# Two-operand elementwise work moved from GpSimd to VectorE in a one-core encoder step

## The chip, the cores and the metric

The kernel runs on one core of one Trainium2 chip. The metric is the device time of one execution in microseconds (us). A core has a matrix engine (TensorE, PE in the profile; its weight loads are the row PEld), three engines for elementwise work (VectorE, DVE; ScalarE, ACT; GpSimd, POOL) and queues for DMA, of which this kernel uses that of SyncE (SP). Each engine executes its own instructions in the order in which the program gives them; semaphores order them between engines.

## The reference, cut to what matters

One inference step of a two-layer streaming encoder on 544 tokens: 512 of a new stream (prompt) and 32 that continue a running one (sample). The width is 1024. Each layer is a half-step gated FFN, a token mixer, and another half-step FFN; layer 0 mixes by retention, layer 1 by differential attention against keys and values that are projected once, after layer 0. Around every sub-layer stand two norms:

```python
h = modulate(x, g_norm[l, 0], mod[:, 0], mod[:, 1])       # rms_norm(x) * g * (1 + scale) + shift
x = x + HALF * mod[:, 2, None] * rms_norm(swiglu(h, w_ffn_in[l, 0], w_ffn_out[l, 0]), g_norm[l, 1])
h = modulate(x, g_norm[l, 2], mod[:, 3], mod[:, 4])
y, st = retention_mixer(h, ...)                           # layer 1: diff_mixer
x = x + mod[:, 5, None] * rms_norm(y, g_norm[l, 3])
h = modulate(x, g_norm[l, 4], mod[:, 6], mod[:, 7])
x = x + HALF * mod[:, 8, None] * rms_norm(swiglu(h, w_ffn_in[l, 1], w_ffn_out[l, 1]), g_norm[l, 5])
```

with `rms_norm(y, g) = y * rsqrt(mean(y * y) + eps) * g`, `swiglu(h) = (silu(a) * b) @ w_out` for `a, b = split(h @ w_in)`, and a rotary embedding on queries and keys: `[x1 * cos - x2 * sin, x2 * cos + x1 * sin]`. The modulations `mod` are products of the conditioning vectors with a large matrix. Everything is float32.

## The kernel before, in words

**Layout.** Activations stand feature-major: 8 tiles of 128 features by 544 tokens in `X`. The tokens are worked in two halves, the first with 256 tokens, the second with 288 (256 of the prompt and the 32 of the sample). A product of one 128-wide column block of a weight matrix with one half is a unit; there are 368 units, each done for both halves.

**Products in three parts.** TensorE multiplies in a fast format (`F32R`) that keeps fewer bits, so both operands are split in a high and a low part, and a unit is three products for each of its 6 or 8 blocks of K: high x high, high x low, low x high (`run_unit`, L604). Weights arrive by DMA on SP's queue into one of three raw buffers (`w_dma`); `w_conv` then *stages* them: ScalarE rounds them to the high part (L581), and a subtraction makes the low part (L585 on VectorE or L586 on GpSimd), which lets the raw buffer go. Four staged buffers (`NW`) exist. 544 stagings serve the 368 units: where both halves use a unit's weights soon after one another they are staged once, otherwise twice.

**What follows a product.** ScalarE and VectorE take it out of PSUM: silu and gate in the FFNs (L926, L927, L930, L939, L942), the split of the result into parts (L906, L907), the sum of the output product over parts (L893, L895), the rotary embedding (`rot`: L997 and L1001 on VectorE with one operand in PSUM, then the addition of the two, L1005, on GpSimd), and in retention two decay multiplications of queries (L1242, L1275, GpSimd).

**Ends of sub-layers** (`sub_end`, `x_norm`). `sq_sum` squares the 8 tiles on ScalarE (L812, L815) and adds them up on VectorE (L817). `rstd` sums over features with TensorE (L709), scales (L713, VectorE), takes the power -1/2 on GpSimd (L715) and spreads it over the partitions with TensorE (L720). Then VectorE scales each tile of y (L854), and the residual addition X + z follows (L859 on GpSimd or L860 on VectorE). The next norm squares and sums the new X alike, and `pre_ops` makes the next operand of it (L747 VectorE, L756 ScalarE, L762 VectorE). Retention and attention take more powers on GpSimd (L1134, L1585).

**The order.** While the program is built, a planner (`Sched`) lays all of it out on an estimated clock. Every piece of work is a small process that asks for an engine with an estimated cost and a priority; an engine that is free by the estimate takes the ready item of the lowest number, and the instruction is emitted at that moment. So each engine's order is fixed before the run. Norms ask with 0 to 2, work after products with 15 to 20, the low part of a staging with `FIN_P = 25`. `plan` puts the units in order: around the ends of sub-layers the first half is some units ahead, so that products of one half run while the norm of the other is worked out.

Two of the items are alternatives (`"ALT"`): offered to two engines at once, with 1000 added to the priority on the second, and done by whichever takes it first. Staging offers its subtraction to VectorE, then GpSimd. The residual addition, reversed by `[::XADD]` with `XADD = -1`, does the same. The planner's cost of a two-operand instruction of n elements is `(64 + n) / 0.96` ns on VectorE and `150 + 2.1 * n` on GpSimd. Its estimate has no term for one engine holding up another.

Of the kernel before, what the change touches and what calls it, by code (L numbers as in the profile page):

```python
# [29 lines left out]

# columns of the constant table
C_ID = 0
# [5 lines left out]
C_N = 220  # L38
# columns of the per-head decay table
T_DM = 0  # L40
# [3 lines left out]

# lead of the first half, delay of a wakeup, staged weights kept free for the products that come next
L0 = 1
# [4 lines left out]
def _path():  # L51
    """Where each half stands: the first one is ahead around the ends of the sub-layers, so that the products of one
    half run while the norms, or the attention, of the other are worked out."""
    p = [((None, L0), (None, 0))]
    for e in ((0, 1), (0, 2), "kv", (1, 0)):
        x, hold, y, z = BND.get(e, BND0)
        p += [((e, -z), (e, -z - L0)), ((e, 0), (e, -x)), ((e, 0), (e, -x + hold)), ((e, y), (e, 0)),
              ((e, y + z), (e, y + z - L0))]
    return p + [((e0, a), (e1, b)) for e0, a, e1, b in ATT]
# [60 lines left out]
class Sched:  # L120
    """Orders the instructions: small processes compete for the engines on an estimated clock."""

# [146 lines left out]

def c_pool(n):  # L270
    return 150 + 2.1 * n


class Operand:
    """A 128 x 544 operand, in two token halves, each split into two float32r parts."""

# [30 lines left out]
class Load:  # L307
    """One staging of a unit's weights, for one token half or for both."""

# [16 lines left out]
def yoco_step(ctx: ExitStack, tc: tile.TileContext, I, O):  # L326
# [68 lines left out]

    def pool(n, fn, pr=None):
        return ("POOL", c_pool(n), fn) if pr is None else ("POOL", c_pool(n), fn, pr)

    def dma(nbytes, out, in_, pr=None, eng=None):
# [3 lines left out]

# [1 line left out]
    ready = {n: Ev() for n in ("ct", "vt", "sc", "lam")}  # L405
# [32 lines left out]

# [1 line left out]
    # modulation m: 0..8 layer 0, 9..10 shared kv, 11..19 layer 1  # L440
    mod_ev = [[Ev() for _ in range(4)] if m < 2 else Ev() for m in range(20)]
# [27 lines left out]
    def ada_first():  # L469
        """The first two modulations, a quarter of their features at a time."""  # L470
        for q in range(4):
# [64 lines left out]
    def derive(i, kind, m, gcol, mul):  # L536
        """DRV[i] = (1 + mod) * g, or (mul * mod) * g"""
        drv_ev[i] = [Ev() for _ in range(4)] if m < 2 else Ev()
# [14 lines left out]

# [1 line left out]
    units = []  # L555
# [15 lines left out]
    def w_conv():  # L571
        for d in loads:
            w = (yield ("get", wpool, 1))[0]
            d.w = w
            yield d.raw_ev
            nk = d.unit.nk
            n = nk * P
            hi = WT[w][:, 0, :nk, :].rearrange("p k f -> p (k f)")
            lo = WT[w][:, 1, :nk, :].rearrange("p k f -> p (k f)")
            src = fa(d.raw)  # L580
            yield act(n, lambda: nc.scalar.copy(hi, src))  # L581

            def fin(d=d, hi=hi, lo=lo, src=src, n=n):
                yield ("ALT", [
                    ("DVE", c_dve(n), lambda: nc.vector.tensor_tensor(lo, src, hi.bitcast(F32), ALU.subtract)),  # L585
                    ("POOL", c_pool(n), lambda: nc.gpsimd.tensor_tensor(lo, src, hi.bitcast(F32), ALU.subtract))])  # L586
                S.put(rawbuf, d.rawbuf)
                S.set(d.staged)
            go(fin(), FIN_P)

# [1 line left out]
    def run_unit(u, H, b):  # L592
# [48 lines left out]
    def plan():  # L641
        """The order of the products along a path of (units of the first half, of the second), and which weights are
        staged twice."""
        marks["end"] = n = len(units)
# [50 lines left out]

# [1 line left out]
    def blocks(H):  # L697
        return ((0, P), (P, P)) if H == 0 else ((0, P), (P, P), (2 * P, NS_TOK))

    def rstd(acc, H, dim, pr=0):  # L700
        """Per-token rstd of the column sums of acc, broadcast over partitions in a PSUM bank."""
        nb, n = (3, 96) if H else (2, P)
# [26 lines left out]
    def pre_ops(H, Rb, n, gi, mi, ops, q=1):  # L729
        """h = x * rstd * gs + shift, split into operands."""  # L730
        if mi:
# [41 lines left out]
    class YBuf:  # L773
        """Holds a sub-layer's y, 8 tiles, while it is accumulated."""

# [23 lines left out]
    def sq_sum(H, src, evs, acc):  # L799
        """acc = sum over the 8 tiles of src squared"""  # L800
        c = COLS[H]
# [32 lines left out]
    def sub_end(H, yevs, gg, nexts, final=False):  # L834
# [10 lines left out]
        for f in range(8):  # L845
# [3 lines left out]
            def one(f=f, ze=ze):  # L849
                z = yield from get(n, -4)  # L850

                def a():
# [4 lines left out]
                S.set(ze)  # L857
                yield ("ALT", [
                    ("POOL", c_pool(n), lambda: nc.gpsimd.tensor_tensor(X[:, f, c], X[:, f, c], fa(z), ALU.add)),  # L859
                    ("DVE", c_dve(n), lambda: nc.vector.tensor_tensor(X[:, f, c], X[:, f, c], fa(z), ALU.add))][::XADD])  # L860
                free(z)
# [20 lines left out]

# [1 line left out]
    def out_stage(w, k0, ops, first, last, yevs):  # L884
# [16 lines left out]
    def split_ops(H, src, op, pr=20):  # L901
        """op = hi, lo of the float32 columns src"""
        c = COLS[H]
# [6 lines left out]
    def ffn(l, j, hops, yevs):  # L910
        w_in, w_out = I["w_ffn_in"][l][j], I["w_ffn_out"][l][j]
        parts = ((0, 8), (8, 16), (16, 22))
        for pi, (f0, f1) in enumerate(parts):
            st = Stage(hops if pi == 2 else [])
            gops = [Operand() for _ in range(f1 - f0)]
            for f in range(f0, f1):
# [3 lines left out]
                def post_a(H, b, sil=sil, sev=sev):  # L920
# [3 lines left out]
                    if l in TANH:  # L924
                        # 2 silu(a) = (1 + tanh(a / 2)) a: tanh shares a table with exp
                        yield act(n, lambda: nc.scalar.activation(fa(t), PS[b][:, :n], AF.Tanh, scale=0.5))  # L926
# [22 lines left out]

# [1 line left out]
    ret = {}  # L951
# [16 lines left out]
    def piece(h, nm):  # L968
        """A buffer of a head, taken by its first use."""
        hd = heads[h]  # L970
# [20 lines left out]
    def rot(H, b, rr, dst, pr=20):  # L991
        """Rotates a projected tile, whose partner rows lie 64 apart, by the table rr."""
        c = COLS[H]
# [10 lines left out]
        put_bank(b)  # L1004
        yield pool(n, lambda: nc.gpsimd.tensor_tensor(dst, a1, a2, ALU.add), pr)  # L1005
        free(t1)
# [99 lines left out]
    def ret_head(h, oo):  # L1106
# [11 lines left out]
        def finish(b, H, c0, n):  # L1118
            """o in bank b, token-major: group norm, gate, split"""
            blks = ((0, P), (P, P)) if n == 256 else ((0, n),)  # L1120
# [114 lines left out]
        def sample():  # L1235
# [5 lines left out]
            c0 = NP_TOK  # L1241
            yield pool(NS_TOK, lambda: nc.gpsimd.tensor_tensor(fa(qs, NS_TOK), V("q")[:, c0:c0 + NS_TOK],  # L1242
                                                               V("t")[:, T_QS:T_QS + NS_TOK], ALU.mult))
            b = yield from bank(miscb)
# [29 lines left out]
        qd = yield from get(256)  # L1274
        yield pool(256, lambda: nc.gpsimd.tensor_tensor(fa(qd), V("q")[:, 256:512], V("t")[:, T_QD:T_QD + 256], ALU.mult))  # L1275
        unpiece(h, "q", "t")
# [16 lines left out]

# [1 line left out]
    kv = {"k": [Ev(2) for _ in range(8)], "v": [Ev(2) for _ in range(8)], "rope_ev": Ev(), "left": 16}  # L1295
# [8 lines left out]
    def to_tok(H, src, h):  # L1304
        """Stores a feature-major tile of the values token-major."""
        b = yield from bank(miscb)
# [49 lines left out]

# [1 line left out]
    at = {}  # L1358
# [131 lines left out]
    def at_block(h, H, ii):  # L1490
        """The queries 128 i .. 128 (i + 1) of a head"""
        i = 2 * H + ii
# [33 lines left out]

        # the first 64 queries don't see the last 64 keys
        def mask():
# [187 lines left out]

# [1 line left out]
    go(setup(), 0)  # L1718
# [4 lines left out]

    # DRV indices: l * 10 + 2 * s (pre of sub-layer s), l * 10 + 2 * s + 1 (post), 6: kv pre
    for l in range(2):
# [25 lines left out]
    for l in range(2):  # L1751
        m0 = 11 * l
        for s in range(3):
            if l or s:
                mark((l, s))
            # the last modulation of this sub-layer and the first ones of the next
            ada_due.append((max(0, len(units) + ADA_LEAD), 6 if l == 0 and s == 2 else (m0 + 3 * s + 4) // 2))
# [30 lines left out]

# [1 line left out]
ROPE_LEAD = 30  # L1790
# [3 lines left out]
W_P = {0: 0.5, 1: 1.5, 2: 2.5}  # L1794
# layers whose silu is worked out by tanh
TANH = (1,)
FIN_P = 25
CONV_P = 3
NEXT_P = 25
XADD = -1  # L1800
ADA_HI = 900
# [8 lines left out]

# [1 line left out]
# Rows of a rotary tile: all first halves of the heads' dimensions, then all second halves.  # L1812
def _rope(d, reps, scale=1.0):
# [43 lines left out]
def _cols(w):  # L1857
    """[.., K, N] -> [.., N / 128, 128 (of K), K / 128 * 128]"""
    *b, K, N = w.shape
# [5 lines left out]
def _pairs(w):  # L1865
    """The columns of each pair of 64-wide heads: both first halves, then both second halves"""
    *b, N = w.shape
# [54 lines left out]
```

## Time and profile before

| what | before |
| --- | --- |
| median of 3 runs | 2639.63 us (2636.75 to 2639.95) |
| span of the profiled execution | 2637.7 us, 1.9 us below that median; no other time is listed for it |
| TensorE busy | 2540.7 us, 96% |
| VectorE busy | 1362.2 us, 52% |
| ScalarE busy | 1037.5 us, 39% |
| GpSimd busy | 425.1 us, 16% |
| staging subtractions | 433 on VectorE (L585), 111 on GpSimd (L586) |
| rotary additions on GpSimd (L1005) | 64, 55.6 us |
| residual additions | 52 on VectorE (L860), 44 on GpSimd (L859) |

Busy times are those of the profiled execution; engines run side by side, so they don't add up to the span. A row of a group gives the source line, the engine, the operation, what it writes and reads, its count, then the busy time and the mean duration of one in ns, then the idle time of the engine just before and what ended it. `FA` is the large scratch area in SBUF, `w` the staged weights, `r` the operands of the products, `ps` PSUM.

### The profile page before, as it was taken

To read this page: it belongs to the slowest core of one execution; us is meant where nothing else is said; L and a number is where in the kernel's file an instruction comes from. 1 tells how busy PE (TensorE), PEld (TensorE's weight loads), DVE (VectorE), ACT (ScalarE), POOL (GpSimd) and SP (SyncE) were. 2 spreads that over 40 slices of the span, in tenths; PEclk is the share of its full clock that TensorE was granted. 3 is DMA by queue.
4 is the path that set the end of the run, shared out by engine and by line. 5 is a ranking of instruction groups with operands and counts; after the bars stand their busy time and mean duration, and the time that the engine had idled before them with its cause. 6 is when DMAs were issued, how large, how long until landed. Compare 5 with 4: busy or idle time off the path is not lost.

```text
span 2637.7 us, 48412 instructions
## 1 busy us (share of the span) xinstructions
PE 2540.7 (96%) x19908; PEld 2399.0 (91%) x19908; DVE 1362.2 (52%) x2481; ACT 1037.5 (39%) x2055; POOL 425.1 (16%) x323
## 2 busy tenths in 40 slices
PE   7999999899999989999999899999999899999998
PEld 5799999799999987899998799999789888889998
DVE  5223336844333365223338734556766966668555
ACT  3222224443323333222224433434554565544433
POOL 1000002422202121000003420000441433322000
PEclk9999999999999999999999999999999999999999
DMA  8722324642222238622225753555664444445553
GB/s 323 270 87 89 97 89 136 225 134 94 76 90 79 75 109 304 221 86 95 88 79 168 257 164 111 169 176 187 237 226 147 139 164 169 160 143 172 168 165 109
DMA packets 119549, 400.57 MB, mean 152 GB/s; under 512 B 13344, under 2 KB 31904, under 8 KB 109088
## 3 DMA queue, kind: packets, MB, share of 16 engines
q1 hardware_dynamic: 119328, 397.48, 44.5%
q8 instruction: 156, 2.56, 0.4%
q14 instruction: 65, 0.53, 0.1%
HBM read 384.19 MB, written 13.24 MB: 151 GB/s over the span
## 4 chain that ended last, share of the span: by engine, by line
PE 82%; DVE 11%; issue 3%; DMA 2%; ACT 1%; POOL 1%; SPq 0%; DVEq 0%; POOLq 0%; ACTq 0%
PE ps L604 73%; DVE FA L817 2%; DVE r L762 2%; PE ps L508 2%; DMA FA<-in_ada 2%; DVE FA L854 1%; PE ps L1524 1%; DVE FA L747 1%; DVE X L860 1%; PE ps L1566 1%; DVE w L585 1%; ACT w L581 1%; DMA X<-in_xb 0%; PE ps L720 0%; PE ps L1197 0%
## 5 line engine op out<-in xcount | busy, mean ns | idle before, releaser
L604 PE MATMUL ps<-r,w 128*128 128x288 f32 (+1 forms) x17280 | 2286.9, 292 | 14.7 <-DVE r L762 6.5
L604 PEld LDWEIGHTS ps<-r,w 128*128 128x128 f32 x17280 | 2216.5, 192 | 83.5 <-issue 56.3
L581 ACT CAST w<-FA 128x1024 fp32r<-128x1024 f32 (+1 forms) x544 | 556.3, 1023 | 907.5 <-PE ps L604 829.1
L585 DVE TENSOR_TENSOR w<-FA,w 128x1024 fp32r<-128x1024 f32 (+1 forms) x433 | 521.7, 1205 | 597.2 <-ACT w L581 596.0
L586 POOL TENSOR_TENSOR w<-FA,w 128x1024 fp32r<-128x1024 f32 (+1 forms) x111 | 262.8, 2369 | 974.3 <-DVE r L907 366.3
L715 POOL TENSOR_TENSOR FA<-FA,NHALF 128x2 f32<-128x2 f32 (+1 forms) x24 | 23.9, 995 | 829.5 <-DVE FA L713 791.8
L942 DVE TENSOR_TENSOR FA<-ps,FA 128x256 f32<-128x256 f32 (+1 forms) x88 | 38.6, 441 | 186.6 <-PE ps L604 184.7
L906 ACT CAST r<-FA 128x256 fp32r<-128x256 f32 (+1 forms) x176 | 73.1, 417 | 129.7 <-DVE FA L942 92.9
L895 DVE TENSOR_TENSOR FA<-ps,FA 128x288 f32<-128x288 f32 (+1 forms) x144 | 62.6, 438 | 102.1 <-PE ps L604 100.8
L817 DVE TENSOR_TENSOR FA<-FA 128x256 f32<-128x256 f32 (+1 forms) x168 | 104.5, 623 | 12.9 <-ACT FA L815 11.7
L907 DVE TENSOR_TENSOR r<-FA,r 128x256 fp32r<-128x256 f32 (+1 forms) x176 | 87.7, 499 | 24.0 <-ACT r L906 23.5
L762 DVE SCALAR_TENSOR_TENSOR r<-FA,MOD,r 128x256 fp32r<-128x256 f32 (+1 forms) x168 | 94.6, 619 | 0.7 <-ACT r L756 0.3
L756 ACT ACTIVATE r<-FA,MOD 128x256 fp32r<-128x256 f32 (+1 forms) x168 | 61.9, 436 | 66.1 <-DVE FA L747 65.8
L508 PE MATMUL ps<-FA,SC 128*32 128x512 f32 x576 | 77.1, 612 | 3.1 <-DMA FA<-in_ada 3.0
L1005 POOL TENSOR_TENSOR FA<-FA 128x256 f32<-128x256 f32 (+1 forms) x64 | 55.6, 869 | 144.2 <-DVE FA L1001 142.0
L939 DVE SCALAR_TENSOR_TENSOR FA<-ps,FA 128x256 f32<-128x256 f32 (+1 forms) x88 | 38.6, 439 | 56.1 <-PE ps L604 55.2
L997 DVE TENSOR_TENSOR FA<-ps,FA 128x256 f32<-128x256 f32 (+1 forms) x64 | 28.0, 438 | 69.9 <-PE ps L604 67.8
L930 ACT ACTIVATE FA<-ps 128x256 f32<-128x256 f32 (+1 forms) x88 | 34.5, 394 | 71.4 <-PE ps L604 69.9
L747 DVE SCALAR_TENSOR_TENSOR FA<-X,DRV,ps 128x256 f32<-128x256 f32 (+1 forms) x168 | 56.3, 395 | 8.9 <-PE ps L720 8.5
L1001 DVE TENSOR_TENSOR FA<-ps,FA 64x256 f32<-64x256 f32 (+1 forms) x128 | 56.1, 438 | 2.3
L709 PEld LDWEIGHTS ps<-ONE,FA 128*32 128x32 f32 x408 | 6.9, 121 | 53.6 <-DVE FA L817 48.9
L815 ACT ACTIVATE FA<-X 128x256 f32<-128x256 f32 (+1 forms) x84 | 33.7, 426 | 53.5 <-DVE X L860 48.0
(147 smaller groups left out, 1271.0 us busy)
## 6 DMA issues: line engine op xcount, KB each, us to landing
FA<-in_w_ffn_in SPq DMA_DIRECT2D x256, 512.0 KB, 3.2
FA<-in_ada SPq DMA_DIRECT2D x80, 1024.0 KB, 6.8
FA<-in_w_ffn_out SPq DMA_DIRECT2D x95, 512.0 KB, 3.5
FA<-in_w_in_a SPq DMA_DIRECT2D x60, 512.0 KB, 3.2
FA<-in_w_ffn_out SPq DMA_DIRECT2D x61, 384.0 KB, 3.1
FA<-in_w_kv SPq DMA_DIRECT2D x22, 512.0 KB, 3.6
FA<-in_w_out_a SPq DMA_DIRECT2D x19, 512.0 KB, 3.3
FA<-in_w_q_b SPq DMA_DIRECT2D x16, 512.0 KB, 3.3
```

The lines of the kernel that those rows point to most:

```text
L508: te.matmul(PS[b][32 * g:32 * g + 32, :], lhsT=SC[:, k, :], rhs=fa(ada_buf[u, k], 512, g * 512), start=(k == 0), stop=(k == 7))
L581: yield act(n, lambda: nc.scalar.copy(hi, src))
L585: ("DVE", c_dve(n), lambda: nc.vector.tensor_tensor(lo, src, hi.bitcast(F32), ALU.subtract)),
L586: ("POOL", c_pool(n), lambda: nc.gpsimd.tensor_tensor(lo, src, hi.bitcast(F32), ALU.subtract))])
L604: te.matmul(PS[b][:, :n], lhsT=w[:, a, k, :], rhs=x, start=(k == 0 and j == 0), stop=(k == u.nk - 1 and j == 2))
L747: nc.vector.scalar_tensor_tensor(fa(z, c1 - c0, o), X[:, f, c0:c1], DRV[:, gi, f, s:s + 1], PS[Rb][:, o:o + c1 - c0], ALU.mult, ALU.mult)
L756: nc.scalar.activation(op.hi(H, c0, c1), fa(z, c1 - c0, o), AF.Identity, bias=MOD[:, mi, f, s:s + 1])
L762: nc.vector.scalar_tensor_tensor(op.lo(H, c0, c1), fa(z, c1 - c0, o), MOD[:, mi, f, s:s + 1], op.hi(H, c0, c1).bitcast(F32), ALU.add, ALU. ...
L817: yield dve(n, lambda: nc.vector.tensor_tensor(acc, acc, fa(t), ALU.add))
L895: yield dvp(n, lambda: nc.vector.tensor_tensor(Y[:, f, c], PS[b][:, :n], Y[:, f, c], ALU.add), 15)
L906: yield act(n, lambda: nc.scalar.copy(op.hi(H), src), pr)
L907: yield dve(n, lambda: nc.vector.tensor_tensor(op.lo(H), src, op.hi(H).bitcast(F32), ALU.subtract), pr)
```

## The change

GpSimd keeps the powers alone. The staging subtraction and the residual addition are no longer offered to two engines but asked of VectorE; the rotary addition and the two decay multiplications of retention go to VectorE with VectorE's cost in the estimate. Priorities stay as they are, and the planner works out a new order with them. Comments are also taken out, which changes line numbers little.

```diff
@@ w_conv
             def fin(d=d, hi=hi, lo=lo, src=src, n=n):
-                yield ("ALT", [
-                    ("DVE", c_dve(n), lambda: nc.vector.tensor_tensor(lo, src, hi.bitcast(F32), ALU.subtract)),
-                    ("POOL", c_pool(n), lambda: nc.gpsimd.tensor_tensor(lo, src, hi.bitcast(F32), ALU.subtract))])
+                yield dve(n, lambda: nc.vector.tensor_tensor(lo, src, hi.bitcast(F32), ALU.subtract))
                 S.put(rawbuf, d.rawbuf)
                 S.set(d.staged)
@@ sub_end
                 S.set(ze)
-                yield ("ALT", [
-                    ("POOL", c_pool(n), lambda: nc.gpsimd.tensor_tensor(X[:, f, c], X[:, f, c], fa(z), ALU.add)),
-                    ("DVE", c_dve(n), lambda: nc.vector.tensor_tensor(X[:, f, c], X[:, f, c], fa(z), ALU.add))][::XADD])
+                yield dve(n, lambda: nc.vector.tensor_tensor(X[:, f, c], X[:, f, c], fa(z), ALU.add))
                 free(z)
@@ rot
-        yield pool(n, lambda: nc.gpsimd.tensor_tensor(dst, a1, a2, ALU.add), pr)
+        yield dve(n, lambda: nc.vector.tensor_tensor(dst, a1, a2, ALU.add), pr)
@@ ret_head, sample
-            yield pool(NS_TOK, lambda: nc.gpsimd.tensor_tensor(fa(qs, NS_TOK), V("q")[:, c0:c0 + NS_TOK],
-                                                               V("t")[:, T_QS:T_QS + NS_TOK], ALU.mult))
+            yield dve(NS_TOK, lambda: nc.vector.tensor_tensor(fa(qs, NS_TOK), V("q")[:, c0:c0 + NS_TOK],
+                                                              V("t")[:, T_QS:T_QS + NS_TOK], ALU.mult))
@@ ret_head
-        yield pool(256, lambda: nc.gpsimd.tensor_tensor(fa(qd), V("q")[:, 256:512], V("t")[:, T_QD:T_QD + 256], ALU.mult))
+        yield dve(256, lambda: nc.vector.tensor_tensor(fa(qd), V("q")[:, 256:512], V("t")[:, T_QD:T_QD + 256], ALU.mult))
```

More of the change, by code (lines that the diff above doesn't have):

```diff
@@ L267, in c_dvp @@
     return (64 + n) / 0.96
-def c_pool(n):
-    return 150 + 2.1 * n
 class Operand:
@@ L394, in dvp @@
         return ("DVE", c_dvp(n), fn) if pr is None else ("DVE", c_dvp(n), fn, pr)
-    def pool(n, fn, pr=None):
-        return ("POOL", c_pool(n), fn) if pr is None else ("POOL", c_pool(n), fn, pr)
     def dma(nbytes, out, in_, pr=None, eng=None):
@@ L1799 @@
 NEXT_P = 25
-XADD = -1
 ADA_HI = 900
```

## The prediction

> **What bounds the kernel now.** I read the page first, then the busy time by stretches, then what TensorE (PE) waited for, and last one sub-layer end in order of time.
>
> ```profile
> span 2637.7 us, 48412 instructions
> PE 2540.7 (96%) x19908; PEld 2399.0 (91%) x19908; DVE 1362.2 (52%) x2481; ACT 1037.5 (39%) x2055; POOL 425.1 (16%) x323
> ```
>
> PE is the bound: 96% of the span. Whatever VectorE (DVE) does while PE streams products costs nothing; the change can only touch the 97 us in which PE is idle. Where are they? Columns: stretch, its length, then busy us (instructions) of PE, PEld, DVE, ACT, POOL, the granted clock, DMA share and GB/s.
>
> ```profile
> 423.00:519.00 96.00, 85.70 (x691) 76.56 (x690) 82.86 (x166) 45.93 (x94) 38.37 (x26) 0.96 0.60 206
> 960.00:1030.00 70.00, 61.46 (x498) 49.24 (x498) 55.07 (x122) 29.98 (x64) 25.94 (x18) 0.93 0.58 205
> 1405.00:1495.00 90.00, 77.60 (x600) 66.72 (x600) 85.96 (x188) 46.50 (x104) 43.08 (x29) 0.94 0.62 217
> 1830.00:1970.00 140.00, 131.88 (x1015) 114.66 (x1014) 104.64 (x236) 80.54 (x218) 54.23 (x43) 0.98 0.68 236
> 2030.00:2110.00 80.00, 69.50 (x560) 67.76 (x560) 73.54 (x139) 40.90 (x82) 39.17 (x24) 0.94 0.41 132
> 2110.00:2300.00 190.00, 186.40 (x1382) 159.88 (x1380) 125.20 (x269) 109.51 (x266) 68.10 (x47) 1.00 0.50 167
> 2360.00:2430.00 70.00, 61.81 (x508) 60.34 (x507) 60.76 (x113) 33.92 (x66) 27.09 (x16) 0.95 0.46 146
> 2430.00:2620.00 190.00, 190.00 (x1439) 190.00 (x1438) 104.61 (x142) 79.61 (x115) 0.00 (x0) 1.00 0.50 160
> ```
>
> Six stretches around the ends of sub-layers hold 10.3 + 8.5 + 12.4 + 8.1 + 10.5 + 8.2 = 58 us of PE idle time. In five of them DVE is 79 to 96% busy and GpSimd (POOL) at work too; the attention (2110 to 2300) loses 3.6 us, the last FFN none. What PE waits for (total us, times, longest):
>
> ```profile
> PE ps L709 <- DVE FA L817: 46.8, 12, 11.9
> PE ps L604 <- DVE r L762: 6.5, 8, 1.5
> PE ps L1559 <- DVE FA L1553: 2.4, 3, 1.5
> PE ps L604 <- POOL w L586: 1.2, 2, 0.9
> PE ps L604 <- DVE w L585: 0.5, 1, 0.5
> ```
>
> L709 sums the squares of a norm and waits for the last L817 add. The longest wait, 11.9 us, is the kernel's start; 34.9 us remain. Weights are hardly ever late (1.7 us). Now DVE's own groups; the last column set is busy us, mean ns.
>
> ```profile
> L762 DVE SCALAR_TENSOR_TENSOR r<-FA,MOD,r 128x256 fp32r<-128x256 f32 x112 | 78.8, 726 | 0.7 <-ACT r L756 0.3
> L817 DVE TENSOR_TENSOR FA<-FA 128x288 f32<-128x288 f32 x84 | 53.5, 637 | 5.4 <-ACT FA L815 4.8
> L747 DVE SCALAR_TENSOR_TENSOR FA<-X,DRV,ps 128x256 f32<-128x256 f32 x112 | 50.1, 473 | 8.9 <-PE ps L720 8.5
> ...
> L860 DVE TENSOR_TENSOR X<-X,FA x52: 408/446/2658, 445.3 to 2633.9; 128x256 f32<-128x256 f32 x31, 128x288 f32<-128x288 f32 x21
> L860 DVE TENSOR_TENSOR X<-X,FA 128x256 f32<-128x256 f32 (+1 forms) x52 | 47.4, 919 | 0.0
> ...
> L817 DVE TENSOR_TENSOR FA<-FA 128x288 f32<-128x288 f32 x4 | 1.8, 452 | 0.6 <-ACT FA L815 0.6
> L585 DVE TENSOR_TENSOR w<-FA,w 128x1024 fp32r<-128x1024 f32 x53 | 65.0, 1226 | 56.3 <-ACT w L581 56.3
> ```
>
> The last two rows are from 2430 to 2620, where POOL does nothing: the 288-wide L817 takes 452 ns there and 637 over the span. L860 has a median of 446, a mean of 919 and a longest of 2658. L747, of the same form as L762 but with one input in PSUM, is not stretched (473 against 726). So a VectorE instruction with both inputs in SBUF is held while POOL works. One sub-layer end shows by how much:
>
> ```profile
> 963.45 2.39 POOL L586 TENSOR_TENSOR w<-FA,w 128x1024 fp32r<-128x1024 f32 x1 [1.49 <-ACT w L581]
> 963.77 2.69 DVE L860 TENSOR_TENSOR X<-X,FA 128x256 f32<-128x256 f32 x2
> ...
> 970.95 5.04 POOL L586 TENSOR_TENSOR w<-FA,w 128x1024 fp32r<-128x1024 f32 x2
> 971.19 2.59 DVE L817 TENSOR_TENSOR FA<-FA 128x256 f32<-128x256 f32 x1
> ...
> 974.10 2.17 DVE L817 TENSOR_TENSOR FA<-FA 128x256 f32<-128x256 f32 x1
> 976.19 0.41 DVE L860 TENSOR_TENSOR X<-X,FA 128x256 f32<-128x256 f32 x1
> ...
> 978.76 0.39 PE L709 MATMUL ps<-ONE,FA 128*32 128x2 f32 x16 [6.36 <-DVE FA L817]
> 979.50 1.23 DVE L585 TENSOR_TENSOR w<-FA,w 128x1024 fp32r<-128x1024 f32 x1
> 979.65 1.64 POOL L715 TENSOR_TENSOR FA<-FA,NHALF 128x2 f32<-128x2 f32 x1 [3.67 <-DVE FA L713]
> ```
>
> An L860 that begins inside POOL's staging ends with it, and so do both L817; then PE stands 6.36 us for the chain of squares.
>
> **The change, part by part.** *Staging.* POOL loses these:
>
> ```profile
> L586 POOL TENSOR_TENSOR w<-FA,w 128x1024 fp32r<-128x1024 f32 x96 | 233.6, 2435 | 316.1 <-ACT w L581 275.4 <-ACT r L1168 15.1 <-DMA out_vp<-FA 8.7
> L586 POOL TENSOR_TENSOR w<-FA,w 128x768 fp32r<-128x768 f32 x15 | 29.2, 1947 | 658.2 <-DVE r L907 366.3 <-DMA FA<-vsc 275.6 <-ACT w L581 16.3
> L1005 POOL TENSOR_TENSOR FA<-FA 128x256 f32<-128x256 f32 (+1 forms) x64 | 55.6, 869 | 144.2 <-DVE FA L1001 142.0 <-PE ps L1149 1.8 <-POOL FA L1005 0.2
> L859 POOL TENSOR_TENSOR X<-X,FA 128x288 f32<-128x288 f32 (+1 forms) x44 | 36.6, 851 | 33.4 <-DVE FA L854 33.2
> ```
>
> On DVE the 96 wide ones cost 1226 ns each, 118 us; the 15 narrow ones three quarters of that (0.92), 14 us. *Rotary additions* (64) and *residual additions* (44) cost what an undisturbed L860 does, 446 ns: 29 + 20 us. The 16 multiplications of retention are bounded by that row too: at most 7 us. Together 188 us more on DVE. *Held time given back*, from the groups above: L762 112 x (726 - 473) = 28; the 288-wide L817 84 x (637 - 452) = 16, its 84 narrower ones by the same difference 16; L860 52 x (919 - 446) = 25: 85 us, and less in other groups. So DVE goes from 1362 to about 1465 us, 55%: still no bound over the span, and in the FFNs PE's products hide it (2430 to 2620 already has every staging on DVE and PE at 100%).
>
> What counts is the six stretches. In the example, from 963.45 to 978.76, the held time is 2.69 - 2 x 0.41 = 1.9 for the L860 pair, 2.59 - 0.41 = 2.2 and 2.17 - 0.41 = 1.8 for the L817: 5.9 us. Three stagings come in their place, 3 x 1.23 = 3.7 us, if they stay inside the chain, and POOL's three residual additions of that stretch, 1.2 us. If all stagings stay inside, the chain gets 5.9 - 4.9 = 1.0 us shorter, 16% of the 6.36 us wait; if all fall behind it, 4.7 us, 74%. A staging has the last priority on DVE (25, against 1 for the norms), so the planner puts it where no norm instruction is ready; but the chain waits for ScalarE's squares between its additions, and there a staging gets in. I take 60%, nearer the second end: of 34.9 us, 21. The planner also knows now when DVE is free, which it didn't when POOL held it, so PE's sums should stand later in its queue, behind products that are ready.
>
> *L762 and L1553*, which PE also waits for (8.9 us), are held alike; at 60%, 5 us. *The tail* loses POOL's help:
>
> ```profile
> 2628.83 2.84 DVE L854 SCALAR_TENSOR_TENSOR FA<-FA,DRV,ps 128x256 f32<-128x256 f32 x10 [2.00 <-PE ps L720]
> 2629.61 4.78 POOL L859 TENSOR_TENSOR X<-X,FA 128x288 f32<-128x288 f32 x6 [1.78 <-DVE FA L854]
> 2633.90 0.80 DVE L860 TENSOR_TENSOR X<-X,FA 128x288 f32<-128x288 f32 x1
> ```
>
> Six additions join DVE after the last product: 6 x 0.45 = 2.7 us at most, less the held part of L860 (0.80 - 0.45) and of its like: 2 us lost. *Weights late*: staging has no second engine when DVE is full; the 1.7 us that PE waits for weights I put at 5 (bounds: nothing, and rival C). *The powers stay on POOL.* The L715 above took 1.64 us beside DVE's L585:
>
> ```profile
> L715 POOL TENSOR_TENSOR FA<-FA,NHALF 128x2 f32<-128x2 f32 x12 | 10.3, 855 | 550.8 <-DVE FA L713 513.1 <-issue 20.1 <-ACT w L581 17.5
> ```
>
> DVE is free while a norm's power is taken, so stagings gather just there. 24 powers, each late by up to 1.64 - 0.86 = 0.8 us: at most 19 us on the chains. The norm chains end at an idle PE in 10 or so cases, and half of those collide: 3 us lost (bounds 0 and 19). The Trainium skill, page "SBUF — State Buffer", section "Who interferes with whom", says that the port pair which GpSimd shares with VectorE is an exclusive lock: whichever instruction starts first keeps it to its end. By that rule the powers can be held by stagings as the stagings held the additions, with one staging's 1.23 us as the most; the row's 0.8 is inside that, and the term would be at most 5 us in place of 3.
>
> No wait is added on a queue, and no DMA is moved; SP's loads start when a staging frees its raw buffer, and DVE's staging frees it 1.2 us sooner than POOL's.
>
> Sum: 21 + 5 - 2 - 3.3 (weights, 5 less 1.7) - 3 = 17.7 us. 2637.7 - 17.7 = 2620.0 for the span; the median of the runs is 1.9 us above the profiled span, so 2622.
>
> **The rivals.** *B, the boundaries close.* The held time was what put PE's sums too early in its queue; with a true plan PE runs the other half's products meanwhile. 91 to 100% of the waits on L817, L762 and L1553 go, 34.9 + 8.9 = 44 us, less 5 for tail and powers: 2601. For it: PE is at 100% in the stretch without POOL. Against it: that stretch has no sub-layer end.
>
> *C, slower: VectorE becomes the bound at the sub-layer ends.* Half of POOL's time there (1226 against 2435 ns) added to DVE's: 82.9 + 19.2 = 102 in 96 us, 86.0 + 21.5 = 107.5 in 90, 73.5 + 19.6 = 93 in 80, 60.8 + 13.5 = 74 in 70: 6 + 17.5 + 13 + 4 = 41 us too much if no held time came back. If half of that remains, through stagings that starve behind the norms (priority 25) until PE has used up its four buffers, 2639.6 + 20 = 2660. It decides from the point at which DVE's work exceeds the stretch. Against it: the held time in the example (5.9 us) exceeded what comes (4.9). The Trainium skill's "Perfetto Trace Analysis", section "Optimizing Scalar/DVE Operations", leans to this side: it would move work to GpSimd where VectorE is saturated, but adds that the shared port may undo it. The rows above show this port's price.
>
> *D, no change.* What comes equals what goes back, as with all stagings inside the chain: 16% of 43.8 is 7 us, less tail, weights and powers, 8: 2640.
>
> **How the numbers follow.** About 0.2%, 5 us, is what a measurement of this kernel tells from no change. My forecast A (2610 to 2633) has 0.47, B 0.15, C 0.23, D 0.15. Faster: A and B with a little of D, 0.63; same 0.14; slower 0.23. The range reaches past most of B and into C: 2594 to 2656.
>
> **What would show it.** DVE's L860, L817 and L762 with means at 0.45, 0.41 to 0.45 and 0.47 us, none near 2.6; DVE near 1465 us; POOL at 60 to 70 us (425.1 - 262.8 - 55.6 - 36.6 = 70, less the multiplications); PE's wait for L817 at 25 us or less, idle time in the six stretches down by some 25 us; the tail 2 us longer. Wrong if PE waits more than 15 us for staged weights (C), if the additions stay stretched (the holder was not POOL's two-operand work), or if the wait for L817 stays at 35 us with DVE full (D).

## The result and the profile after

The changed kernel takes 2663.05 us (median of 4 runs, 2657.99 to 2668.01) against 2639.79 us: a ratio of 1.0093, 95% interval 1.0077 to 1.0109. It is slower by 23 us, outside the range that the prediction gave. The profiled execution took 2668.0 us, the slowest of the four, and its span is 2666.2. Lines of the program after the change stand up to 12 lower: L604 is L595 now, L585 and L586 are L577, L709 is L700, L715 is L706, L720 is L711, L762 is L753, L817 is L808, L860 and L859 are L849, L907 is L896, L927 is L916, L1005 is L994, L1553 is L1542, L1559 is L1548.

The page of the changed kernel, busy us, share and instructions:

```profile
span 2666.2 us, 48255 instructions
PE 2558.3 (96%) x19908; PEld 2409.8 (90%) x19908; DVE 1402.8 (53%) x2716; ACT 1040.3 (39%) x2055; POOL 65.3 (2%) x88
```

The two profiled executions end 28.5 us apart. Only 10.9 us of that is time in which TensorE idles (107.9 us after, 97.0 before). The other 17.6 us is TensorE's busy time for the same 19908 instructions, at a mean granted clock of 0.977 against 0.987.

VectorE took over 184 us of work (132 of stagings, 27 of rotary additions, 20 of residual ones, 5 of multiplications) and is only 41 us busier. The groups of VectorE by shape show why: their instructions are no longer stretched.

```profile
L753 DVE SCALAR_TENSOR_TENSOR r<-FA,MOD,r 128x256 fp32r<-128x256 f32 x112 | 51.6, 480 | 8.9 <-ACT r L747 8.8
L808 DVE TENSOR_TENSOR FA<-FA 128x288 f32<-128x288 f32 x84 | 38.1, 454 | 6.8 <-ACT FA L806 6.3
...
L849 DVE TENSOR_TENSOR X<-X,FA x96: 417/438/455, 444.6 to 2662.9; 128x256 f32<-128x256 f32 x48, 128x288 f32<-128x288 f32 x48
```

The first went from 726 ns to 480, the second from 637 to 454; the slowest of the 96 residual additions takes 455 ns, where the slowest before took 2658. The longest L753 takes 487 ns and the longest L808 460, so no held time is left in these groups.

And TensorE ran ahead with it. The busy time of the products alone, for the first 2000 us, of the kernel before and then of the changed one:

```profile
0.00:2000.00 2000.00, 1753.03 (x13302) 1700.83 (x13303) 0.99 0.44 151
```

```profile
0.00:2000.00 2000.00, 1774.38 (x13567) 1723.79 (x13568) 1.00 0.46 154
```

By then the changed kernel has done 265 products more. At 1753 us for 13302 of them, 0.13 us each, that is a lead of 35 us. The loss of 23 us is what is left of this lead when 58 us are lost after it. The stretches of the changed kernel:

```profile
423.00:519.00 96.00, 88.34 (x716) 75.48 (x714) 79.50 (x188) 45.59 (x93) 4.62 (x5) 0.96 0.69 241
960.00:1030.00 70.00, 66.60 (x540) 51.00 (x540) 53.97 (x140) 32.28 (x68) 2.44 (x3) 0.98 0.78 290
1390.00:1480.00 90.00, 83.67 (x671) 70.36 (x670) 83.77 (x207) 46.91 (x99) 4.57 (x4) 0.96 0.79 271
1810.00:1950.00 140.00, 138.63 (x1087) 123.94 (x1086) 116.85 (x275) 84.55 (x224) 11.32 (x18) 1.00 0.66 228
2000.00:2080.00 80.00, 61.32 (x447) 59.62 (x446) 61.39 (x143) 35.04 (x70) 6.01 (x3) 0.83 0.34 111
2245.00:2350.00 105.00, 80.34 (x422) 58.19 (x421) 42.95 (x115) 38.39 (x114) 6.53 (x11) 0.76 0.23 76
2385.00:2455.00 70.00, 59.06 (x459) 57.73 (x457) 52.65 (x116) 31.79 (x60) 3.87 (x2) 0.88 0.46 143
```

The first four ends of sub-layers idle 7.7, 3.4, 6.3 and 1.4 us in place of 10.3, 8.5, 12.4 and 8.1. The fifth and the sixth (the last row) went the other way, 18.7 for 10.5 and 10.9 for 8.2. And a stretch that idled 3.6 us in 190 before, the attention, now idles 24.7 us in 105, with a VectorE that is 41% busy: nothing there is short of an engine. The products that are left in it are mostly small ones of the attention, and the granted clock in it is 0.76, where the attention had 1.00 before. Where the attention of the second half stands is seen by its L1553 (32 in all), one per block of queries; first before, then after (L1542):

```profile
2110.00:2150.00 40.00, 1.99 (x3) 1.00 0.54 178
2150.00:2230.00 80.00, 4.76 (x7) 1.00 0.49 167
2230.00:2310.00 80.00, 6.20 (x6) 0.96 0.46 153
```

```profile
2100.00:2150.00 50.00, 4.10 (x6) 1.00 0.41 128
2150.00:2230.00 80.00, 0.00 (x0) 1.00 0.61 201
2230.00:2350.00 120.00, 6.84 (x10) 0.79 0.27 85
```

After six blocks the attention of the prompt stops for 80 us, while TensorE spends products of the last FFN's first half and works on the sample. Then ten blocks are left and nothing to cover them.

What TensorE waited for in the changed kernel:

```profile
PE ps L700 <- DVE FA L808: 27.9, 8, 11.7
PE ps L595 <- DVE w L577: 18.2, 9, 5.2
PE ps L1548 <- DVE FA L1542: 10.9, 6, 3.0
PE ps L711 <- POOL FA L706: 10.8, 7, 3.2
```

The sums of squares wait 16.2 us beside the start (27.9 - 11.7), where it was 34.9. Staged weights, 1.7 us before, are waited for 18.2 us, and the powers of the norms 10.8 us (L720 before: 1.5).

### The profile page after: what moved, and what is told of

It reads as the page before. It is cut to its first block, busy times and chain, and to the rows that moved or that the text cites. A ratio compares the mean times of both kernels' runs of the same rounds, so it can differ in the third digit from the quotient of the medians.

```text
span 2666.2 us, 48255 instructions
## 1 busy us (share of the span) xinstructions
PE 2558.3 (96%) x19908; PEld 2409.8 (90%) x19908; DVE 1402.8 (53%) x2716; ACT 1040.3 (39%) x2055; POOL 65.3 (2%) x88
## 5 line engine op out<-in xcount | busy, mean ns | idle before, releaser
L595 PE MATMUL ps<-r,w 128*128 128x288 f32 (+1 forms) x17280 | 2279.6, 292 | 22.8 <-DVE w L577 18.2
L595 PEld LDWEIGHTS ps<-r,w 128*128 128x128 f32 x17280 | 2215.1, 192 | 86.3 <-issue 50.6
L577 DVE TENSOR_TENSOR w<-FA,w 128x1024 fp32r<-128x1024 f32 (+1 forms) x544 | 649.1, 1195 | 601.0 <-ACT w L574 599.3
L884 DVE TENSOR_TENSOR FA<-ps,FA 128x288 f32<-128x288 f32 (+1 forms) x144 | 63.2, 440 | 103.3 <-PE ps L595 101.2
L896 DVE TENSOR_TENSOR r<-FA,r 128x256 fp32r<-128x256 f32 (+1 forms) x176 | 76.8, 437 | 23.2 <-ACT r L895 23.2
L808 DVE TENSOR_TENSOR FA<-FA 128x256 f32<-128x256 f32 (+1 forms) x168 | 73.3, 437 | 13.3 <-ACT FA L806 12.1
L706 POOL TENSOR_TENSOR FA<-FA,NHALF 128x2 f32<-128x2 f32 (+1 forms) x24 | 27.6, 1151 | 1818.9 <-DVE FA L704 1321.2
L928 DVE SCALAR_TENSOR_TENSOR FA<-ps,FA 128x256 f32<-128x256 f32 (+1 forms) x88 | 38.6, 440 | 55.8 <-PE ps L595 55.8
L753 DVE SCALAR_TENSOR_TENSOR r<-FA,MOD,r 128x256 fp32r<-128x256 f32 (+1 forms) x168 | 59.0, 402 | 8.9 <-ACT r L747 8.8
L845 DVE SCALAR_TENSOR_TENSOR FA<-FA,DRV,ps 128x256 f32<-128x256 f32 (+1 forms) x144 | 50.0, 398 | 5.8 <-PE ps L711 5.6
L882 ACT COPY FA<-ps 128x288 f32<-128x288 f32 (+1 forms) x96 | 36.5, 381 | 40.0 <-PE ps L595 40.0
L806 ACT ACTIVATE FA<-FA 128x256 f32<-128x256 f32 (+1 forms) x84 | 35.7, 428 | 31.7 <-DVE FA L884 31.2
L1513 PE MATMUL ps<-FA 128*128 128x128 f32 (+3 forms) x128 | 43.7, 469 | 1.7 <-ACT FA L1496 0.9
```

What stands on the lines that cost most here:

```text
L577: yield dve(n, lambda: nc.vector.tensor_tensor(lo, src, hi.bitcast(F32), ALU.subtract))
L595: te.matmul(PS[b][:, :n], lhsT=w[:, a, k, :], rhs=x, start=(k == 0 and j == 0), stop=(k == u.nk - 1 and j == 2))
L753: nc.vector.scalar_tensor_tensor(op.lo(H, c0, c1), fa(z, c1 - c0, o), MOD[:, mi, f, s:s + 1], op.hi(H, c0, c1).bitcast(F32), ALU.add, ALU. ...
L808: yield dve(n, lambda: nc.vector.tensor_tensor(acc, acc, fa(t), ALU.add))
L884: yield dvp(n, lambda: nc.vector.tensor_tensor(Y[:, f, c], PS[b][:, :n], Y[:, f, c], ALU.add), 15)
L896: yield dve(n, lambda: nc.vector.tensor_tensor(op.lo(H), src, op.hi(H).bitcast(F32), ALU.subtract), pr)
```

## The experiments

Two things were open: whether VectorE can't carry the work, or the new order is at fault; and what stops the attention. A planner makes the order, so the two can be parted: an instruction can be left where the old plan had it and be issued on another engine.

**The old order, all two-operand work on VectorE.** The alternatives, costs and places stay; five times `nc.gpsimd` becomes `nc.vector`.

```diff
-                    ("POOL", c_pool(n), lambda: nc.gpsimd.tensor_tensor(lo, src, hi.bitcast(F32), ALU.subtract))])
+                    ("POOL", c_pool(n), lambda: nc.vector.tensor_tensor(lo, src, hi.bitcast(F32), ALU.subtract))])
```

and so for L859, L1005, L1242 and L1275.

> The planner is left as in the kernel before, with its alternatives and both costs, so every instruction is emitted at the place it had before; but the two-operand work that the plan gives to GpSimd is issued on VectorE. No re-planning, no hold by GpSimd's two-operand work. Theory 1 (the hold was worth some 20 to 40 us, and the changed kernel lost it again by the new plan alone): 2600 to 2625 us, TensorE's wait of L709 for L817 at half of 46.8 us or less. Rival (VectorE can't carry the work at the sub-layer ends whatever the order): 2650 us or more, long waits for staged weights. Rival (the plan is out of step with VectorE's queue, and what is won at one end is lost at another): within 5 us of 2640.

Measured: 2616.4 us, a ratio of 0.9919 (0.9905 to 0.9932). VectorE carries it: the same move that cost 23 us under the new plan gains 21 under the old one.

```profile
PE ps L709 <- DVE FA L817: 37.3, 13, 11.0
PE ps L604 <- DVE r L762: 4.6, 8, 1.4
PE ps L604 <- DVE w L585: 0.5, 1, 0.5
```

The weights are as good as never late. L709's wait is not halved, as theory 1 had it; it falls from 46.8 to 37.3. TensorE idles 80.7 us in place of 97.0, and its busy time falls by 7.7 us (2533.0), at a clock of 0.990.

**The changed kernel, the sample's scratch asked for earlier.** The heads of the attention hold their buffers until the 32 tokens of the sample are done too, three heads at a time. The sample's first pair asks for one stretch of 2992 columns of scratch. On the planner's own clock, worked out while the program is built, this request waits 34 us in the changed kernel and not at all in the one before.

```diff
         hds = [at["hd"][2 * p + j][1] for j in range(2)]
+        if p == 0:
+            yield hds[0].q
+            at["smem"] = yield from get(1056 + 1024 + 576 + 64 + 16 + 2 * P, -2)
         for hd in hds:
             yield hd.ld
         yield ("get", at["ssem"], 1, p)
-        if p == 0:
-            at["smem"] = yield from get(1056 + 1024 + 576 + 64 + 16 + 2 * P, -2)
```

> The changed kernel, with one request moved: the attention of the sample asks for its 2992 columns of scratch as soon as the queries of its first head are there, instead of after the loads of two heads. Theory 1 (the stretch of idle TensorE in the attention, 24.7 us from 2245 to 2350, and its trail come from a late grant of that scratch, which holds all later heads): that idle time goes, about 30 to 40 us less than the changed kernel, 2623 to 2633 us, so faster than before. Rival (VectorE is too slow for the attention): within 8 us of the changed kernel's 2663 us, and TensorE still idle in the attention.

Measured: 2618.4 us, 0.9921 (0.9908 to 0.9935). 45 us are back, more than the 30 to 40 expected, and the changed kernel is faster than the one before, with all of its work on VectorE. Two stretches of the attention, and the wait for weights:

```profile
2080.00:2200.00 120.00, 120.00 (x918) 107.31 (x917) 83.59 (x168) 66.06 (x152) 5.06 (x9) 1.00 0.52 169
2200.00:2320.00 120.00, 120.00 (x921) 105.64 (x920) 78.62 (x165) 64.56 (x153) 6.51 (x11) 1.00 0.50 163
...
PE ps L595 <- DVE w L577: 17.4, 8, 5.2
```

TensorE never idles in these two stretches, and VectorE is busier there (66 to 70%) than in the idle stretch above. The wait for weights is untouched, so it is a loss of its own. Up to 2080 us the two runs go alike: TensorE has done 15964 instructions in the changed kernel and 15972 here, VectorE 2069 in both. So, as far as these counts show, the new plan that this edit brings makes no difference ahead of the attention.

The stretch that idled 24.7 us doesn't make 45 us alone. Of the 49.2 us between the two spans, 27.4 are idle time of TensorE and 21.8 are its busy time for the same 19908 instructions, with a mean clock of 0.986 in place of 0.977. Whether the idle time is what lowered the clock was not tried by itself.

**The same request in pieces**, asked for where the changed kernel asks:

```diff
-            at["smem"] = yield from get(1056 + 1024 + 576 + 64 + 16 + 2 * P, -2)
+            at["smem"] = []
+            for k in (1056, 512, 512, 576, 64 + 16 + 2 * P):
+                r = yield from get(k, -2)
+                at["smem"].append(r)
```

> The changed kernel; the sample's scratch is asked for at the same point as there, but as five pieces of at most 1056 columns instead of one of 2992. Theory (what was missing was a contiguous stretch): the planner grants it 13 us after the loads instead of 34, and the run comes out like the one that asks earlier, 2613 to 2628 us. Rival (there was no room at all): over 2650 us.

Measured: 2617.8 us, 0.9927 (0.9909 to 0.9946). On the planner's clock the last piece is granted 13 us after the request. There was room earlier, though not in one stretch.

**The kernel before, the sample made late.** The reverse, with GpSimd at work as before: the sample waits for both blocks of queries of the third head (`oev`).

```diff
         yield ("get", at["ssem"], 1, p)
         if p == 0:
+            yield at["hd"][2][1].oev
             at["smem"] = yield from get(1056 + 1024 + 576 + 64 + 16 + 2 * P, -2)
```

> The kernel before, all engines as before; only the sample's attention starts its first pair of heads after both blocks of the third head (half 1) are done, which the planner's clock puts 35 us later, as the late scratch did in the changed kernel. Theory (the late start of the sample is enough for the loss, with no work on VectorE moved): some 35 to 45 us slower than before, 2673 to 2685 us, TensorE idle in the attention. Rival (it takes VectorE's extra work as well): 2640 to 2655 us.

Measured: 2674.1 us, 1.0141 (1.0119 to 1.0162), 36 us slower. What TensorE waits for in the attention is as in the changed kernel (L1559 for L1553, 10.9 us there, 2.4 in the kernel before):

```profile
PE ps L1559 <- DVE FA L1553: 11.9, 8, 3.0
```

Up to 2080 us this run and the kernel before have done the same 15853 instructions of TensorE. The late start alone makes such a loss; no work has to move for it.

**The changed kernel, the staging's priority at 1.2.**

```diff
-FIN_P = 25
+FIN_P = 1.2
```

> The changed kernel with the staging's priority at 1.2 instead of 25, and nothing else: the sample's scratch is still asked for late. Theory (two separate losses, which add up: late scratch some 45 us, starving stagings some 20 us): 2635 to 2650 us, with the idle stretch of the attention still there. Rival (the priority alone closes that stretch too): under 2625 us.

Measured: 2642.4 us, 1.0015 (1.0005 to 1.0026): 21 us less than the changed kernel, and the attention still idles (2200 to 2320):

```profile
2200.00:2320.00 120.00, 99.61 (x611) 77.11 (x612) 58.59 (x143) 48.98 (x136) 7.05 (x12) 0.87 0.31 100
...
PE ps L595 <- DVE w L577: 0.7, 2, 0.4
```

**Both edits.**

> The run with the scratch asked for earlier, and the staging's priority at 1.2 instead of 25, among the norms' own. Theory (stagings that starve behind the norms cost TensorE the 18.2 us that it waits for L577 in the changed kernel): 8 to 18 us less than the run with the scratch alone, 2608 to 2622 us. Rival (a staging put ahead of the norms delays their chains by as much): within 5 us of that run, with the wait for the last addition of squares grown by what the wait for weights lost.

Measured: 2596.7 us, 0.9843 (0.983 to 0.9857), the fastest of all, and faster than expected (2608 to 2622). The two losses add up: 2663.1 - 45 (scratch) - 21 (priority) = 2597. Its waits:

```profile
PE ps L700 <- DVE FA L808: 14.5, 3, 11.6
PE ps L595 <- DVE FA L916: 9.3, 3, 4.4
...
PE ps L711 <- POOL FA L706: 4.9, 4, 1.8
PE ps L595 <- ACT FA L806: 4.8, 3, 1.7
PE ps L595 <- DVE FA L884: 3.9, 1, 3.9
PE ps L595 <- DVE FA L928: 3.9, 1, 3.9
...
PE ps L595 <- DVE w L577: 0.4, 1, 0.4
```

Beside the start, the norms' sums now wait 2.9 us, and the powers 4.9 in place of 10.8. So stagings put first don't make TensorE wait longer for the norm chains. Some 22 us of wait are new, at the gate of an FFN (L916, L928), at squares (L806) and at the sum of an output product (L884). Why the norms' sums wait less was not tried.

**Which part gains.** Three more runs in the old order. The stagings alone:

> The kernel before with its plan; only the 111 staging subtractions that the plan gives to GpSimd are issued on VectorE; the rotary and residual additions stay where they were. Theory 1 (the 2.4 us stagings are what holds VectorE): most of the gain of the run with all on VectorE, 2605 to 2628 us. Rival (the small additions hold it as much, or the staging on VectorE costs the norm chains what the hold did): 2635 us or more.

Measured: 2601.6 us, 0.9865 (0.985 to 0.988), better than the theory's range. VectorE does 132 us of stagings more and is only 7.6 us busier (1369.8): these 111 instructions had held it for some 124 us, most of the 143. The small ones alone:

> The kernel before with its plan; the 111 stagings stay on GpSimd, and the rotary and residual additions and the two multiplications that the plan gives to GpSimd are issued on VectorE. The stagings alone on VectorE gained 36 us, all on VectorE 21 us, so the small ones should cost some 15 us. Theory (their hold is short, and each of them lengthens VectorE's chains more than the hold did): 2640 to 2660 us. Rival (what the additions cost depends on the stagings being there too): 2625 to 2638 us.

Measured: 2640.3 us, 1.0012 (1.0002 to 1.0022): nothing to speak of, at the lower end of the theory's range but without the 15 us that it set out from. VectorE takes over 52 us of work and is 52.8 us busier (1415.0): no held time comes back. The small instructions, now on VectorE, are held there themselves by the stagings that are still on GpSimd. Here are the rotary additions of this run, then of the run with all on VectorE:

```profile
L1005 DVE TENSOR_TENSOR FA<-FA 128x256 f32<-128x256 f32 (+1 forms) x64 | 56.6, 888 | 0.8
```

```profile
L1005 DVE TENSOR_TENSOR FA<-FA 128x256 f32<-128x256 f32 (+1 forms) x64 | 27.6, 435 | 0.5
```

They take 888 ns instead of 435, and on GpSimd they took 869. So without the stagings the small ones neither gain nor cost the 15 us. They do cost it when the stagings are on VectorE too, and the residual additions are most of it:

> The kernel before with its plan; stagings and residual additions on VectorE, rotary additions and multiplications on GpSimd. It lies between the run with the stagings alone (2601.6 us) and that with all (2616.4 us). Theory (the residual additions stand in the norm chains for which TensorE waits, the rotary ones mostly do not): 2608 to 2618 us, most of the 15 us. Rival (the rotary additions cost as much): 2601 to 2608 us.

Measured: 2614.7 us, 0.9916 (0.9903 to 0.993), 13 of the 15 us. The groups of that run show the work undisturbed (L860 at 437 ns, L859 on VectorE at 442), so it isn't a hold:

```profile
L860 DVE TENSOR_TENSOR X<-X,FA 128x256 f32<-128x256 f32 (+1 forms) x52 | 22.4, 437 | 0.0
L859 DVE TENSOR_TENSOR X<-X,FA 128x288 f32<-128x288 f32 (+1 forms) x44 | 19.4, 442 | 0.0
...
PE ps L709 <- DVE FA L817: 37.8, 13, 11.6
```

L709 waits 37.8 us, against 31.5 with the stagings alone. That the old plan places these additions for two engines, and one then does them in a row, is a possible reason that was not shown; a plan that knows of it was the next run.

**Re-planned, stagings on VectorE first, small additions as before.** Both edits from above on the kernel before, with only the staging taken from GpSimd.

> Re-planned: stagings on VectorE alone at priority 1.2, the sample's scratch asked for earlier, but the residual additions still offered to both engines and the rotary additions on GpSimd. Theory (the small additions are better off on GpSimd): 2580 to 2595 us, the fastest so far. Rival (their hold costs as much as they save VectorE): 2595 to 2603 us, like the run with all on VectorE and the same two edits (2596.7 us).

Measured: 2604.5 us, 0.9872 (0.9856 to 0.9889), a little above the rival's range as well. The theory falls: once the plan knows where the additions are, GpSimd's help with them gains nothing in this plan; the run is 8 us behind the one with all on VectorE.

| kernel | us | ratio to before |
| --- | --- | --- |
| changed | 2663.1 | 1.0093 |
| changed, staging first | 2642.4 | 1.0015 |
| changed, scratch earlier / in pieces | 2618.4 / 2617.8 | 0.9921 / 0.9927 |
| changed, scratch earlier, staging first | 2596.7 | 0.9843 |
| old order, all / staging and residual / staging | 2616.4 / 2614.7 / 2601.6 | 0.9919 / 0.9916 / 0.9865 |
| old order, small additions | 2640.3 | 1.0012 |
| staging first, scratch earlier, small ones as before | 2604.5 | 0.9872 |
| before, sample late | 2674.1 | 1.0141 |

## Why the prediction was wrong, point by point

**The sum against the runs.** Without the two losses below the changed kernel is 41 us faster than the one before (2596.7 against 2637.9), more than the 17.7 that was forecast. With them (45 and 21 us) it is 23 slower.

**Held time given back: right, and more.** The prediction took 85 us from four groups "and less in other groups". VectorE's 1362 + 184 - 1403 = 143 us says that 143 came back. So VectorE ended at 1403 us and not at 1465.

**The sums of squares: right in size.** 21 us off L709's wait were forecast; 34.9 - 16.2 = 18.7 came. In the same run TensorE was 35 us ahead after 2000 us. That the size came out is in part luck: in the old order, where VectorE's additions are not stretched either (L817 434 ns on average), the wait fell by 9.5 us only, so the rest came with the new plan, which is not parted further.

**L762 and L1553: half right.** 5 us were forecast. The wait for L762 fell from 6.5 to 1.2 us; that for L1553 rose from 2.4 to 10.9, in the attention that had lost its cover.

**The tail: right in size.** From the end of TensorE's last product to the end of the span it is 10.3 us after 8.9, 1.4 longer for the 2 that were forecast.

**The step that failed: a new plan was costed as if only the moved instructions changed.** The prediction put the attention down as losing 3.6 us and left it out of the sum ("What counts is the six stretches"); under "No wait is added on a queue" it looked at queues and not at what the planner itself hands out, scratch above all. A different order frees buffers at different moments, and one request for 2992 columns in one stretch was granted late. That holds the heads of the attention, which hold back the last units. 45 us are shown by taking it away in two ways, and 36 by putting it into the kernel before. No term of the sum, and no rival, had a place for it.

**A premise that failed: only TensorE's idle time can change.** The prediction set out from "the change can only touch the 97 us in which PE is idle". Idle time rose by 10.9 us and the busy time of the same instructions by 17.6, with a lower mean clock (0.977 for 0.987).

**Weights late: mis-sized.** The sum went from 1.7 us to 5; TensorE waited 18.2 us, and the priority alone is worth 21. "A staging has the last priority" was read as good for the norm chains only. It was the other side that decided: GpSimd had taken 111 of the 544 stagings, and with that way out gone they came late behind the norms.

**Powers: mis-sized.** 3 us were taken, with up to 0.8 us for one; TensorE waited 10.8 us where it had waited 1.5, and one power took 3.17 us, 2.3 more than the 0.85 of an undisturbed one. The bound came from the one collision in view, with a single staging.

**The small additions.** That they cost VectorE 446 ns each was right (418 to 454). That they gain when moved was assumed with the rest: they gain nothing by themselves, as the stagings left on GpSimd hold them, and 13 of the old order's 36 us go when the residual ones move with the stagings.

**Rival C came near in number (2660) by another way.** Its sign, over 15 us of wait for weights, is there. The half of its mechanism in which stagings starve behind the norms is real, and worth 21 us. The other half, a VectorE that is full at the sub-layer ends, is not what made the kernel slower: with the scratch earlier the waits for weights stay (17.4 us) and the kernel is 0.8% faster than before. In the first four stretches TensorE idled less, as forecast; in the fifth and the sixth, where single waits for weights reached 4.9 and 5.2 us, more.

## What to carry to other kernels

Where an order comes from a planner, moving an instruction is two changes, the engine's time and a new plan; issue it on the new engine at its old place first, and the two can be told apart in one run. If a kernel gets slower, look for the stretch in which no engine is busy (here VectorE at 41% beside an idle TensorE): that points to a buffer or a semaphore, and not to an engine. Moving only the short instructions off an engine gains nothing while the long ones that stay there hold them on their new one. And work that had two engines to go to had a priority that suited two: with one of them gone, the priority has to be set again.

## What the runs showed of the hardware that was not expected

The hold works both ways, and in these traces GpSimd did not get its turn between two of VectorE's instructions. At the sixth sub-layer end of the changed kernel:

```profile
2390.83 0.41 DVE L896 TENSOR_TENSOR r<-FA,r 128x256 fp32r<-128x256 f32 x1
2391.05 3.17 POOL L706 TENSOR_TENSOR FA<-FA,NHALF 96x3 f32<-96x3 f32 x1 [13.93 <-DVE FA L704]
2391.16 2.35 DVE L577 TENSOR_TENSOR w<-FA,w 128x1024 fp32r<-128x1024 f32 x2
2394.28 1.60 PE L711 MATMUL ps<-CT,FA 96*128 96x96 f32 x6 [0.88 <-POOL FA L706]
```

A power of three columns, recorded from 2391.05, ends only after a split (L896) and two whole stagings that follow one another: 3.17 us. The Trainium skill's "SBUF — State Buffer", "Who interferes with whom", has an exclusive lock that whoever starts first keeps for the whole instruction; by it one of VectorE's instructions should be the most that GpSimd waits for. The trace shows a wait through more than one here, 2.3 us of it against the 1.23 of a single staging. It is not a single case: five of the 24 powers of this run took 1.9 to 3.2 us, and each ended 0.6 to 0.7 us after the last of a row of two or more such VectorE instructions. Why the lock wasn't passed on in between was not tried.
